# Half of the first layer's embedding projection, made at the end of attention

## The chip, the cores and the metric

The kernel runs on one core of a Trainium2 chip. The metric is the device time of one execution in microseconds (us). Before the change three runs took 1222.86 to 1224.16 us, median 1223.41 us.

## The reference

Two layers over 512 tokens of width 1024, all in fp32. The first layer mixes with forgetting attention (16 heads of 64), the second with a short gated convolution; each is followed by a squared-ReLU MLP and by a gated embedding.

```python
for i in range(DEPTH):                       # DEPTH = 2
    g = norm_g[i]
    hn = rmsnorm(x, g[0])
    m = fox_attention(hn, ...) if i % 2 == 0 else short_conv(hn, ...)
    x = x + rmsnorm(m, g[1])
    f = sq_relu_mlp(rmsnorm(x, g[2]), w_mlp_up[i], w_mlp_down[i])
    x = x + rmsnorm(f, g[3])
    gate = jax.nn.sigmoid(rmsnorm(x, g[4]) @ w_ple_gate[i])
    e = (p[i] @ w_ple_proj[i]) * gate        # p[i]: 512 x 256, w_ple_proj[i]: 256 x 1024
    x = x + rmsnorm(e, g[5])
```

The change concerns `p[i] @ w_ple_proj[i]` for i = 0. It depends on inputs alone.

## The kernel before

Tokens are cut into four blocks of 128 (t) and the width into two halves of 512 columns (n). Every fp32 product is made of three matmuls on operands split into a high and a low part: `mm3` issues high x high (L266), high x low (L267) and low x high (L268). A split is a cast on ScalarE (ACT, L274) and a subtraction on VectorE (DVE, L275) or GpSimd (POOL); of a weight it gives `wh` and `wl`, which are pages.

All buffers in SBUF of 128 x 512 fp32 come from one pool of 70 pages. Results of matmuls go to eight PSUM banks of 128 x 512. Weights are read in one planned order (`plan`): `fetch` issues the load on SyncE's queue into one of 14 `raw` buffers, and `prepare` splits. `wide(key, soon=n)` gives a split weight and sees that the n that come after it in the plan are split as well.

Which instruction stands where in an engine's queue is decided by a scheduler when the program is built; each queue is then worked through in that order. In some stretches the order is that of the code (`manual_schedule`).

The stages of the first layer that matter here:

- *Attention.* For each head, score matmuls (`sc`, L542) are turned into probabilities on DVE, ACT and POOL; these are turned by TensorE (PE) into `pT` (L561), split into `ph` (ACT) and `pl` (DVE), and mixed with the values into `ps_o` (L583, L584). When a head is done, ACT copies half of its bank (`o`, L588) and DVE adds the other half into `oT` (L589); `oT` is later split into `hTh` and `hTl`. A loop over c issues the turn of piece c, the mix of piece c - LAG, and the scores of a piece that is SCORED later; between these it takes steps from a generator, `stream`, which fills TensorE: first the query and key projections of the later heads (`project`, 16 steps for each of seven, 112 in all), then 28 steps of the output projection (`out_part`, one `mm3` each). `share` says how many steps are to be done by piece c; LEFT = 10 steps stay for after the loop.
- *Output projection, MLP.* The rest of the output projection (`o`) and its norm follow, then the MLP (`up`, `dn`), in which TensorE has no gap.
- *The gate's stage* (`ple`). `proj(t, n)` makes one block of p times its weights: six matmuls (`pp`) into a bank. The first four of the eight blocks in BLOCKS, (0,0), (1,0), (0,1), (1,1), are made ahead of the gate matmuls (`early`), while the last results of the MLP are normed and turned (`n_p`, L325). For each block then come 24 gate matmuls (`pg`), a sigmoid on ACT, `proj` if it was not early, the product `e` on DVE (L1069), squares, gain and residual; after both halves of a block its next norm begins, and the second layer's conv (`c`, `u`, `b`) follows.

Of the kernel before, what the change touches and what calls it, by code (L numbers as in the profile page):

```python
# [17 lines left out]
S = 512  # L18
# [8 lines left out]
LAG = 2  # L27
# [53 lines left out]
def trunk(ctx: ExitStack, tc, g4T, x, xT, pT, g, g0T, wv, wqk, bf, wo, wci, wcs, wcb, cw, wco, wup, wdn, wpp, wpg, out):  # L81
# [13 lines left out]
    def bank(name):  # L95
        return psum.tile([P, S], F32, tag="ps", name=name)
# [15 lines left out]
    def plan(key, src):  # L112
        where[key] = len(order)
        order.append((key, len(loads)))
        loads.append(src)
# [60 lines left out]
    def wide(*key, soon=SOON):  # L176

        prepare(where[key] + 1 + soon)
        return ready[key]

    behind = {}
    sums_w = {n: dram.tile([3, P, 2 * S], F32, tag=f"ws{n}", name=f"ws{n}") for n in SUMS_W}

    sum_steps = [(name, kind, i) for name, kind in SUM_STEPS for i in range(3)]
# [21 lines left out]
    for l in range(2):  # L206
        if l == 0:
            for c, (_, width) in enumerate(V_CHUNKS):
                for k in range(KT * width // 512 if width < 272 else KT):
                    plan(("v", c, k), wv[c][k])  # L210
            for i in range(KT):
                for j in range(4):
                    plan(("qk", i, j), wqk[i, j])
            for k in range(KT):
                for n in range(2):
                    plan(("o", n, k), wo[n, k])
        else:
            for s, key in enumerate((("cu", 0), ("b", 0), ("cu", 1))):
                for j in range(4):
                    plan((*key, j), wci[s, j])  # L220
            for i in range(2, KT, 2):
                for _, _, n in PARTS:
                    src = sums_w[n] if n in sums_w else wcs[QUARTERS.index(n)]
                    for s in range(2):
                        plan(("sq", i, s, n), src[i // 2 - 1][:, s * S : (s + 1) * S])
                for j in range(4):
                    plan(("b", i, j), wcb[i // 2 - 1, j])
            for n in range(2):
                for k in range(KT):
                    plan(("co", n, k), wco[n, k])  # L230
        for gr in range(8):
            for i in range(2):
                for j in range(4):
                    plan(("up", l, 2 * gr + i, j), wup[l, 2 * gr + i, j])
            if gr < 7:
                plan_down(l, gr)
                continue
            for n in range(2):
                for f in range(4):
                    plan(("dn", l, gr, n, f), wdn[l, n, 4 * gr + f])  # L240
        for k in range(2):
            plan(("p", l, k), pT[l, :, k, :])
        for n in range(2):
            for k in range(2):
                plan(("pp", l, n, k), wpp[l, n, k])
        for n in range(2):
            for k in range(KT):
                plan(("pg", l, n, k), wpg[l, n, k])
# [130 lines left out]
    def tokens_of(pair, t):  # L379
        return pair.at(lambda h: h[:, t * P : (t + 1) * P])  # L380
# [26 lines left out]
    def attention(hT, first_xT, g0_col, first_x, by_hand):  # L407
# [201 lines left out]
        def out_part(ts, ks):  # L609

            streaming.clear()
            split_o()
            for k in ks:
                for t in ts:
                    for n in range(2):
                        if (t, n) not in banks_o:
                            banks_o[t, n] = bank(f"o{n}_{t}")
                        w = wide("o", n, k, soon=O_SOON)
                        mm3(banks_o[t, n], tokens(oT[0], k, t), w, k == 0, False)
                        yield  # L620

        def stream():
            for i in range(1, KT):
                yield from project(i)
            yield from out_part((0,), range(6))
            yield from out_part((1,), range(6))
            prepare(where["o", 1, KT - 1] + 1)
            yield from out_part((0, 1), (6,))
# [90 lines left out]
        for c in range(-SCORED, n_sc + LAG):  # L719
            if c == n_sc - BY_HAND:  # L720
                by_hand.enter_context(tc.manual_schedule(engines={E.PE}))
            last = n_sc - SCORED - 8
            share = (
                2 * (c + SCORED + 1) if c < last
                else 112 + (c - last + 1) * (28 - LEFT) // (SCORED + 7 + LAG)
            )
            while done < max(share + AHEAD, min(share + STACK, 112)):
                next(main, None)
                done += 1
            if 0 <= c < n_sc:  # L730
                turn(c // 4, c % 4)
            if c >= LAG:
                mix((c - LAG) // 4, (c - LAG) % 4)
            if c % 2 == 0 and c + SCORED < n_sc:
                scores((c + SCORED) // 8, (c + SCORED) % 8 // 2)
            for h in range(2, H):
                if c == 8 * (h // 2) - SCORED - (7 if h % 2 == 0 else 4):
                    bias(h)
# [271 lines left out]
    def ple(l, hT, xs, rs, gB, then):  # L1010
        def proj(t, n):
            pe = bank(f"pp{l}_{n}_{t}")
            for k in range(2):
                mm3(
                    pe, tokens_of(wide("p", l, k), t),
                    wide("pp", l, n, k), k == 0, k == 1,
                )
            return pe
# [29 lines left out]
                )  # L1048
                then(t, at, q)

        early = [proj(t, n) for t, n in BLOCKS[:EARLY]]
        mgs, sums = {}, {}
        for t, n in BLOCKS:
            need(t)
            if (t, n) == (2, 0):
                prepare(where["pg", l, 1, KT - 1] + 1 + SOON)
            pe = early.pop(0) if early else None
            if l == 1 and (t, n) == BLOCKS[-1]:
                last(t, n, mgs[t, 1 - n], sums[t, 1 - n])
                break  # L1060
            ps = bank(f"pg{l}_{n}_{t}")
            for k in range(KT):
                w = wide("pg", l, n, k, soon=soon(t, n))
                mm3(ps, tokens(hT, k, t), w, k == 0, k == KT - 1)
            gate = page(f"gate{l}_{n}_{t}")
            nc.scalar.activation(gate[:, :S], ps, AF.Sigmoid, scale=rs[t])
            pe = pe or proj(t, n)
            e = page(f"e{l}_{n}_{t}")
            nc.vector.tensor_tensor(out=e[:, :S], in0=pe, in1=gate[:, :S], op=ALU.mult)  # L1069
            sums[t, n] = squares(e[:, :S], f"es{l}_{n}_{t}")  # L1070
            mgs[t, n] = gained(e[:, :S], gB, n, f"em{l}_{n}_{t}")
            if (t, 1 - n) in mgs:
                residual(t, *([d.pop((t, i)) for i in range(2)] for d in (mgs, sums)), xs[t],
                         f"er{l}")
                if l == 0:
                    sum_weights()
                then(t)
                if l == 0:
                    sum_weights()
# [145 lines left out]
```

## Time and profile before

| | |
|---|---|
| three runs | 1222.86 to 1224.16 us, median 1223.41 us |
| profiled execution | 1221.69 us, span of its instructions 1220.0 us |
| busy in the span | PE 1207.2, DVE 899.1, ACT 692.1, POOL 658.7 us |
| mean granted TensorE clock | 0.999 |
| attention, up to the last mixing matmul | to 221.2 us |
| rest of the output projection | to 253 us |
| first MLP | 253 to 587.6 us |
| gate's stage of the first layer | 587.7 to 646.6 us |

Rows of the timeline give the start in us from the span's beginning, the length in us, engine, line and operation, tiles (out<-in) and shape, and in brackets how long the engine sat idle before and what ended that. Rows of windows give for a stretch its length, then the busy time and count of PE, PE's weight loads, DVE, ACT and POOL, the granted clock, the DMA share and GB/s. Rows of a tile give the line, engine, operation, count, the least, middle and greatest length in ns, the first and last start, and the shapes.

### The profile page before, as it was taken

Reading aid. Unit: us, or ns where it says so; the run is one execution under the profiler, and the core shown is the slowest. Engines: PE = TensorE matmul, PEld = TensorE weight load, DVE = VectorE, ACT = ScalarE, POOL = GpSimd, SP = SyncE. Lnnn points to the kernel's source line nnn. Section 1 sums busy time; section 2 is a strip of 40 time slices with the busy share of each in tenths; the row PEclk is TensorE's granted clock in tenths of the full one; section 3 lists DMA queues with packets and bytes.
Section 4 is the critical chain, followed back from the end, with each engine's and each line's share of the span. In section 5 each row is a group of like instructions: output and inputs, shape, how many; then the busy total and the mean of one; then the engine's idle time right before and its main releaser. Section 6 shows DMA issues by size and latency. Waiting matters only on the chain.

```text
span 1220.0 us, 18646 instructions
## 1 busy us (share of the span) xinstructions
PE 1207.2 (99%) x6200; PEld 1030.9 (84%) x6200; DVE 899.1 (74%) x1380; ACT 692.1 (57%) x1424; POOL 658.7 (54%) x674
## 2 busy tenths in 40 slices
PE   9999999999999999999999999999999999999997
PEld 8888887898888888888889999889888888888886
DVE  5668888675679776879757877656777687669953
ACT  7567887558634563456756544345756445645641
POOL 3057666167887788775311000028777878678220
PEclk9999999999999999999999999999999999999999
DMA  9554442622365656538345344622422343235401
GB/s 312 192 175 133 128 132 63 218 96 81 104 190 155 156 133 174 161 95 268 105 138 131 111 151 151 192 96 70 138 74 83 120 139 99 67 112 184 144 18 52
DMA packets 90417, 162.90 MB, mean 134 GB/s; under 512 B 10704, under 2 KB 17920, under 8 KB 90128
## 3 DMA queue, kind: packets, MB, share of 16 engines
q1 hardware_dynamic: 86528, 148.85, 38.3%
q0 software_dynamic: 3648, 12.58, 4.8%
q8 instruction: 49, 0.80, 0.3%
q14 instruction: 48, 0.39, 0.1%
q10 hardware_dynamic: 144, 0.26, 0.1%
HBM read 155.29 MB, written 18.96 MB: 143 GB/s over the span
## 4 chain that ended last, share of the span: by engine, by line
PE 95%; DVE 2%; ACT 2%; issue 1%; POOL 0%; POOLq 0%; DVEq 0%; ACTq 0%
PE up L267 9%; PE up L268 9%; PE up L266 9%; PE dn L268 9%; PE dn L266 8%; PE dn L267 8%; PE pg L268 2%; PE pg L266 2%; PE pg L267 2%; PE qk L266 2%; PE qk L267 2%; PE qk L268 2%; PE sq L268 2%; PE sq L267 2%; PE sq L266 2%; PE sc L542 1%
## 5 line engine op out<-in xcount | busy, mean ns | idle before, releaser
L275 DVE TENSOR_TENSOR wl<-raw,wh 128x512 fp32r<-128x512 f32 (+1 forms) x390 | 365.5, 982 | 28.4 <-ACT wh L274 24.3
L274 ACT CAST wh<-raw 128x512 fp32r<-128x512 f32 (+1 forms) x390 | 212.8, 618 | 10.0 <-DMA raw<-in_wv 3.7
L267 PE MATMUL up<-hTl,wh 128*128 128x512 f32 (+1 forms) x576 | 209.9, 366 | 0.0
L266 PE MATMUL up<-hTh,wh 128*128 128x512 f32 (+1 forms) x576 | 209.3, 366 | 0.0
L268 PE MATMUL up<-hTh,wl 128*128 128x512 f32 (+1 forms) x576 | 209.0, 365 | 0.0
L275 POOL TENSOR_TENSOR wl<-T,wh 128x512 fp32r<-128x512 f32 x112 | 157.5, 1438 | 25.9 <-ACT wh L274 24.6
L903 ACT ACTIVATE r<-up 128x512 f32<-128x512 f32 (+1 forms) x72 | 39.4, 547 | 197.0 <-PE up L268 197.0
L951 DVE TENSOR_TENSOR acc<-dn,acc 128x512 f32<-128x512 f32 x168 | 107.8, 678 | 34.7 <-PE dn L268 34.7
L267 PEld LDWEIGHTS up<-hTl,wh 128*128 128x128 f32 x576 | 108.6, 189 | 17.4
L266 PEld LDWEIGHTS up<-hTh,wh 128*128 128x128 f32 x576 | 108.3, 189 | 17.7
L268 PEld LDWEIGHTS up<-hTh,wl 128*128 128x128 f32 x576 | 108.6, 189 | 17.4
L149 POOL TENSOR_TENSOR T<-raw,raw 128x512 f32<-128x512 f32 x56 | 88.5, 1593 | 55.6 <-DMA raw<-in_wdn 23.4
L149 POOL TENSOR_TENSOR T<-raw,T 128x512 f32<-128x512 f32 x56 | 90.7, 1619 | 2.2
L296 POOL TENSOR_SCALAR cor_r_v<-cos,cos 128x1 f32<-128x1 f32 x4 | 1.6, 396 | 152.5 <-ACT junk L308 152.5
L274 ACT CAST wh<-T 128x512 fp32r<-128x512 f32 x112 | 61.4, 616 | 7.0 <-POOL T L149 7.0
L275 DVE TENSOR_TENSOR A11l<-q,A11h 128x256 fp32r<-128x256 f32 x28 | 27.3, 976 | 40.3 <-ACT A11h L274 40.3
L275 DVE TENSOR_TENSOR A12l<-q,A12h 128x512 fp32r<-128x512 f32 x28 | 26.4, 943 | 39.6 <-ACT A12h L274 39.6
L958 POOL TENSOR_TENSOR acc<-acc,acc 128x512 f32<-128x512 f32 x28 | 47.0, 1712 | 10.0 <-DVE acc L951 10.0
L266 PE MATMUL pg<-wh,hTh 128*128 128x512 f32 (+1 forms) x136 | 51.9, 381 | 0.0
L268 PE MATMUL pg<-wh,hTl 128*128 128x512 f32 (+1 forms) x136 | 51.4, 378 | 0.0
L267 PE MATMUL pg<-wl,hTh 128*128 128x512 f32 (+1 forms) x136 | 51.3, 377 | 0.0
L266 PE MATMUL qk<-hTh,wh 128*128 128x512 f32 x128 | 50.9, 398 | 0.0
(318 smaller groups left out, 3267.6 us busy)
## 6 DMA issues: line engine op xcount, KB each, us to landing
raw<-in_wup SPq DMA_DIRECT2D x128, 256.0 KB, 2.8
raw<-in_wdn SPq DMA_DIRECT2D x128, 256.0 KB, 2.8
wst<-in_wcs POOLq DMA_DIRECT2D x18, 512.0 KB, 5.4
raw<-in_wqk SPq DMA_DIRECT2D x32, 256.0 KB, 4.8
raw<-in_wpg SPq DMA_DIRECT2D x32, 256.0 KB, 3.7
raw<-wst SPq DMA_DIRECT2D x24, 256.0 KB, 3.0
g<-in_g SPq DMA_DIRECT2D x18, 256.0 KB, 6.0
raw<-in_wcs SPq DMA_DIRECT2D x18, 256.0 KB, 2.9
```

What stands on the lines that cost most here:

```text
L149: nc.gpsimd.tensor_tensor(out=B[name, p], in0=B[a, p], in1=B[b, p], op=ALU.subtract)
L266: nc.tensor.matmul(ps, a.hi, b.hi, start=start, stop=False)
L267: nc.tensor.matmul(ps, a.hi, b.lo, start=False, stop=False)
L268: nc.tensor.matmul(ps, a.lo, b.hi, start=False, stop=stop)
L274: nc.scalar.copy(hi, src)
L275: eng.tensor_tensor(out=lo, in0=src, in1=hi.bitcast(F32), op=ALU.subtract)
L296: nc.gpsimd.tensor_scalar(out=v, in0=parts[0], scalar1=parts[1], scalar2=EPS, op0=ALU.add, op1=ALU.add)
L542: nc.tensor.matmul(ps[:, :nm], at[:, b * P : n], to[:, :nm], start=s == 0, stop=s == 1)
L903: nc.scalar.activation(r[:, :n], ps[:, :n], AF.Relu)
L951: nc.vector.tensor_tensor(out=a, in0=banks[s], in1=a, op=ALU.add)
L958: nc.gpsimd.tensor_tensor(out=a, in0=a, in1=acc[i, s][:, :S], op=ALU.add)
```

## The change

The four blocks of the second half (n = 1) of the first layer's p times weights are made by a new generator, `embed_part`, as eight more steps of `stream` between the last `project` and the output projection. Each block gets a bank `ppa`, and ACT copies it into a page `ahead`, which is kept until the gate's stage. There the product `e` reads the page, and `early` holds only (0,0) and (1,0); (2,1) and (3,1) no longer call `proj`. For this p is loaded and split a second time, and the two weight tiles of the half stand in the plan ahead of the output projection's. `share` counts eight more steps up to the end of the loop; LEFT is unchanged.

```diff
@@ the plan
                 for j in range(4):
                     plan(("qk", i, j), wqk[i, j])
+            for k in range(2):
+                plan(("pa", l, k), pT[l, :, k, :])
+            for k in range(2):
+                plan(("ppa", l, 1, k), wpp[l, 1, k])
             for k in range(KT):
                 for n in range(2):
                     plan(("o", n, k), wo[n, k])
...
         for n in range(2):
             for k in range(2):
-                plan(("pp", l, n, k), wpp[l, n, k])
+                if l or n == 0:
+                    plan(("pp", l, n, k), wpp[l, n, k])
@@ attention
+        def embed_part():
+
+            streaming.clear()
+            split_o()
+            for t in range(NB):
+                ps = bank(f"ppa_{t}")
+                for k in range(2):
+                    mm3(
+                        ps, tokens_of(wide("pa", 0, k, soon=O_SOON), t),
+                        wide("ppa", 0, 1, k, soon=O_SOON), k == 0, k == 1,
+                    )
+                    yield
+                ahead[t, 1] = page(f"ahead{t}")
+                nc.scalar.copy(ahead[t, 1][:, :S], ps)
+
         def stream():
             for i in range(1, KT):
                 yield from project(i)
+            yield from embed_part()
             yield from out_part((0,), range(6))
...
             share = (
                 2 * (c + SCORED + 1) if c < last
-                else 112 + (c - last + 1) * (28 - LEFT) // (SCORED + 7 + LAG)
+                else 112 + (c - last + 1) * (36 - LEFT) // (SCORED + 7 + LAG)
             )
-            while done < max(share + AHEAD, min(share + STACK, 112)):
+            while done < max(share + AHEAD, min(share + STACK, 120)):
@@ ple
-        early = [proj(t, n) for t, n in BLOCKS[:EARLY]]
+        early = {(t, n): proj(t, n) for t, n in BLOCKS[:EARLY] if (l, n) != (0, 1)}
...
-            pe = early.pop(0) if early else None
+            pe = early.pop((t, n), None)
+            if l == 0 and n == 1:
+                pe = ahead.pop((t, n))[:, :S]
...
-            pe = pe or proj(t, n)
+            if pe is None:
+                pe = proj(t, n)
```

The scheduler orders both programs anew. Lines of the changed kernel are higher by 5 in the helpers and in attention up to the new function (L266 is now L271, L542 is L547), and by more behind it. Three places show what moved.

TensorE's queue at the end of attention, before, at the scores of the seventh pair of heads (`pT_1` is the turn of a piece of an earlier head, `ps_o` the mix):

```order
L542 MATMUL sc_2_2796<-kh_6_2233,q_6_2230 128x384
L542 MATMUL sc_2_2796<-kl_6_2234,q_6_2230 128x384
L561 MATMUL pT_1_2833<-ident,pr_2097 128x128
L561 MATMUL pT_1_2833<-ident,prr_2099 128x128
L561 MATMUL pT_1_2833<-ident,prl_2098 128x128
L583 MATMUL ps_o_2733<-ph_2_2729,v_2_175 128x256
L584 MATMUL ps_o_2733<-pl_2_2730,v_2_175 128x256
L561 MATMUL pT_2_2846<-ident,prr_2099 128x128
L561 MATMUL pT_2_2846<-ident,prl_2098 128x128
L583 MATMUL ps_o_2733<-ph_3_2764,v_2_179 128x256
L584 MATMUL ps_o_2733<-pl_3_2765,v_2_179 128x256
L583 MATMUL ps_o_2853<-ph_0_2789,v_2_167 128x512
```

The same place of the change:

```order
L547 MATMUL sc_2_2796<-kh_6_2233,q_6_2230 128x384
L547 MATMUL sc_2_2796<-kl_6_2234,q_6_2230 128x384
L271 MATMUL ppa_2841<-wh_2306,wh_2238 128x512
L272 MATMUL ppa_2841<-wl_2307,wh_2238 128x512
L273 MATMUL ppa_2841<-wh_2306,wl_2239 128x512
L271 MATMUL ppa_2841<-wh_2328,wh_2263 128x512
L272 MATMUL ppa_2841<-wl_2329,wh_2263 128x512
L273 MATMUL ppa_2841<-wh_2328,wl_2264 128x512
L588 MATMUL ps_o_2733<-ph_2_2729,v_2_175 128x256
L589 MATMUL ps_o_2733<-pl_2_2730,v_2_175 128x256
L566 MATMUL pT_1_2848<-ident,pr_2097 128x128
L566 MATMUL pT_1_2848<-ident,prr_2099 128x128
```

The first block of six stands directly behind the scores; a second stands between the mixes with `ph_3` and `pl_3` of the same head, and the third and fourth follow within the 42 rows that begin with the first `ppa`. The output projection's first matmul stood six rows behind the last row shown of before's queue; now it stands 37 rows behind the last `ppa`.

ACT's queue at the same place, before:

```order
L274 CAST ph_1_2837<-pT_1_2833 128x384
L588 COPY o_2843<-ps_o_2733 64x512
L552 ACTIVATE prr_2514,sm_2_2809<-prr_2514,nmx_2_2808 128x384
L274 CAST ph_2_2849<-pT_2_2846 128x256
L274 CAST hTh<-oT_2585 128x512
L552 ACTIVATE prl_2400,sm_3_2864<-prl_2400,nmx_3_2863 128x512
L552 ACTIVATE prl_2513,sm_3_2871<-prl_2513,nmx_3_2870 128x512
L274 CAST ph_3_2897<-pT_3_2895 128x128
```

and of the change:

```order
L279 CAST ph_1_2852<-pT_1_2848 128x384
L593 COPY o_2858<-ps_o_2733 64x512
L557 ACTIVATE prr_2514,sm_2_2809<-prr_2514,nmx_2_2808 128x384
L640 COPY ahead_2863<-ppa_2841 128x512
L279 CAST ph_2_2875<-pT_2_2872 128x256
L279 CAST hTh<-oT_2585 128x512
L640 COPY ahead_2903<-ppa_2865 128x512
L557 ACTIVATE prl_2400,sm_3_2890<-prl_2400,nmx_3_2889 128x512
L640 COPY ahead_2922<-ppa_2905 128x512
L279 CAST ph_3_2914<-pT_3_2912 128x128
L279 CAST ph_0_2933<-pT_0_2928 128x512
L557 ACTIVATE prl_2513,sm_3_2897<-prl_2513,nmx_3_2896 128x512
```

Three of the four copies stand among the casts and exponentials of three heads, and the second `prl` exponential has moved behind two casts; the fourth copy stands nine rows further.

TensorE's queue at the start of the gate's stage, before, at the end of the early blocks:

```order
L268 MATMUL pp_1_1_7238<-wh_6923,wl_6855 128x512
L325 MATMUL n_p_0_7242<-ident,xd_1_0_6778 128x128 x4
L266 MATMUL pp_1_1_7238<-wh_6935,wh_6866 128x512
L325 MATMUL n_p_1_7249<-ident,xd_1_1_6780 128x128 x4
L267 MATMUL pp_1_1_7238<-wl_6936,wh_6866 128x512
L268 MATMUL pp_1_1_7238<-wh_6935,wl_6867 128x512
L266 MATMUL pg_0_0_7259<-wh_6957,hTh 128x512
L267 MATMUL pg_0_0_7259<-wl_6958,hTh 128x512
```

and of the change:

```order
L273 MATMUL pp_0_1_7284<-wh_6938,wl_6915 128x512
L271 MATMUL pp_0_1_7284<-wh_6950,wh_6926 128x512
L272 MATMUL pp_0_1_7284<-wl_6951,wh_6926 128x512
L273 MATMUL pp_0_1_7284<-wh_6950,wl_6927 128x512
L271 MATMUL pg_0_0_7291<-wh_6983,hTh 128x512
L272 MATMUL pg_0_0_7291<-wl_6984,hTh 128x512
L330 MATMUL n_p_0_7307<-ident,xd_1_0_6838 128x128 x4
L330 MATMUL n_p_1_7314<-ident,xd_1_1_6840 128x128 x4
```

The gate's first matmul stands twelve matmuls nearer to the MLP's last, and the turn of the second token block, which stood among the early blocks, now stands behind the gate's second matmul.

More of the change, by code (lines that the diff above doesn't have):

```diff
@@ L179, in wide @@
         return ready[key]
-    behind = {}
+    behind, ahead = {}, {}
     sums_w = {n: dram.tile([3, P, 2 * S], F32, tag=f"ws{n}", name=f"ws{n}") for n in SUMS_W}
```

## The prediction

> **What bounds the kernel now.** I read the head of the page, then the chain of waits, then TensorE's own timeline, because the first two name one engine and the third says how full it really is.
>
> ```profile
> span 1220.0 us, 18646 instructions
> PE 1207.2 (99%) x6200; PEld 1030.9 (84%) x6200; DVE 899.1 (74%) x1380; ACT 692.1 (57%) x1424; POOL 658.7 (54%) x674
> PE 95%; DVE 2%; ACT 2%; issue 1%; POOL 0%; POOLq 0%; DVEq 0%; ACTq 0%
> ```
>
> TensorE (PE) carries 95% of the chain. A change that only moves matmuls can therefore win only what TensorE loses somewhere, and the busy sum seems to leave 12.8 us over the whole span. But a matmul's row is longer than the room it takes. In a stretch where nothing is waited for:
>
> ```profile
> 195.11 0.28 PE L542 MATMUL sc<-kh,q 128*128 128x256 f32 x1
> 195.47 0.28 PE L542 MATMUL sc<-kl,q 128*128 128x256 f32 x1
> 204.35 0.27 PE L561 MATMUL pT<-ident,pr 128*128 128x128 f32 x1
> 204.46 0.27 PE L561 MATMUL pT<-ident,prr 128*128 128x128 f32 x1
> 222.60 0.39 PE L266 MATMUL o<-wh,hTh 128*128 128x512 f32 x1
> 226.00 0.39 PE L266 MATMUL o<-wh,hTh 128*128 128x512 f32 x1
> ```
>
> Fifteen matmuls of 512 columns start between 222.60 and 226.00, so one takes 0.227 us of the engine, though its row says 0.39. Likewise a 256-column one takes 0.12 (three steps in 0.36) and a transpose 0.11; for 384 columns I estimate 0.175, halfway between 0.12 and 0.227. So a gap up to about 0.16 us long behind a matmul counts as busy, and I count starts instead. The place that matters is the end of attention, from the last matmul ahead of the new ones (184.3) to the last mixing matmul (221.2):
>
> ```profile
> 184.30:221.30 37.00, 35.25 (x191) 27.86 (x190) 29.92 (x82) 27.05 (x67) 20.48 (x36) 1.00 0.15 47
> L266 PE MATMUL o<-wh,hTh x20: 387/393/478, 188.9 to 220.1; 128*128 128x512 f32 x20
> L267 PE MATMUL o<-wl,hTh x20: 389/394/501, 189.1 to 220.3; 128*128 128x512 f32 x20
> L268 PE MATMUL o<-wh,hTl x20: 389/394/481, 189.4 to 220.5; 128*128 128x512 f32 x20
> L542 PE MATMUL sc<-kh,q x11: 281/367/411, 183.9 to 201.7; 128*128 128x512 f32 x4, 128*128 128x256 f32 x4, 128*128 128x384 f32 x3
> L542 PE MATMUL sc<-kl,q x11: 283/332/398, 184.1 to 202.0; 128*128 128x512 f32 x4, 128*128 128x256 f32 x4, 128*128 128x384 f32 x3
> L561 PE MATMUL pT<-ident,prl x23: 270/272/328, 184.8 to 219.6; 128*128 128x128 f32 x23
> L561 PE MATMUL pT<-ident,prr x22: 270/272/327, 184.7 to 217.5; 128*128 128x128 f32 x22
> L561 PE MATMUL pT<-ident,pr x11: 270/273/328, 184.5 to 217.0; 128*128 128x128 f32 x11
> L583 PE MATMUL ps_o<-ph,v x26: 274/364/504, 184.8 to 221.0; 128*128 128x256 f32 x14, 128*128 128x512 f32 x6, 128*128 128x384 f32 x6
> L584 PE MATMUL ps_o<-pl,v x26: 278/361/470, 185.0 to 221.1; 128*128 128x256 f32 x14, 128*128 128x512 f32 x6, 128*128 128x384 f32 x6
> ```
>
> The first row's columns after the length are busy time and count of PE, weight loads, DVE, ACT and POOL. Of 512 columns there are 60 + 8 + 12 = 80, of 256 28 + 8 = 36, of 384 12 + 4 = 16 (the two at 183.9 and 184.1 lie before), of 128 56. Room needed: 80 x 0.227 + 36 x 0.12 + 16 x 0.175 + 56 x 0.11 = 31.4 us of 36.9. TensorE loses **5.5 us** here, where its busy row admits 1.75. DVE and ACT are busy 81% and 73%: this is the stretch in which TensorE waits for the softmax pieces. One cluster can be seen directly:
>
> ```profile
> 185.22 0.27 PE L561 MATMUL pT<-ident,prl 128*128 128x128 f32 x1
> 185.51 0.39 PE L583 MATMUL ps_o<-ph,v 128*128 128x256 f32 x1
> 186.25 0.36 PE L584 MATMUL ps_o<-pl,v 128*128 128x256 f32 x1 [0.35 <-DVE pl L275]
> 187.35 0.50 PE L583 MATMUL ps_o<-ph,v 128*128 128x512 f32 x1 [0.74 <-ACT ph L274]
> ```
>
> Start to start 0.29, 0.74 and 1.10 where 0.11, 0.12 and 0.12 would do: 1.8 us lost in three steps.
>
> The Trainium skill, "Trainium Kernel Development and Optimization", section "Performance Expectations", says that matmul busy time is a bad metric, since matmuls are pipelined. The trace agrees (0.39 against 0.227); by the busy row the change could gain 1.75 us at most, by starts 5.5.
>
> **The change, part by part.** *Removed from the gate's stage:* four blocks of six matmuls, two at its start and two inside. 24 x 0.227 = **5.4 us** of TensorE. Is the stage TensorE's?
>
> ```profile
> 587.60:646.60 59.00, 59.00 (x282) 49.16 (x282) 38.62 (x59) 36.00 (x79) 16.35 (x26) 1.00 0.36 105
> 587.66 0.39 PE L266 MATMUL pp<-wh,wh 128*128 128x512 f32 x1
> 593.99 0.39 PE L266 MATMUL pg<-wh,hTh 128*128 128x512 f32 x1
> 590.40 0.68 DVE L275 TENSOR_TENSOR hTl<-n_p,hTh 128x512 fp32r<-128x512 f32 x1
> 600.04 1.42 DVE L368 SCALAR_TENSOR_TENSOR xd<-acc,mr_r_y,xd 128x512 f32<-128x512 f32 x2 [0.85 <-POOL mr_r_y L303]
> 605.14 1.03 PE L325 MATMUL n_p<-ident,xd 128*128 128x128 f32 x8
> 646.59 0.28 PE L266 MATMUL c<-hTh,wh 128*128 128x256 f32 x1
> ```
>
> Yes: between 587.66 and 646.59 the starts follow without a gap worth naming, and DVE and ACT have a third of it free. Two covers get thinner. The early blocks end 2.7 us sooner, at about 590.4; the gate's first matmul then needs the first half of the turned tokens, whose second half is complete at 590.40 + 0.68 = 591.1 and is asked for four weight tiles (4 x 0.68 us) later. And the turn of the last token block, at 605.14 before and at 605.3 after (counting the room of the rows ahead of it in the new order), needs a DVE row that is finished at 601.5. Neither becomes late, so the whole 5.4 us leaves this stage, and conv begins 5.4 us earlier.
>
> *Added at the end of attention:* the same 24 matmuls, 5.4 us of TensorE, in the stretch that loses 5.5. The new order puts them into 42 rows that begin directly ahead of the cluster above, twelve of them before the matmuls that waited there, so its 1.8 us are filled for certain. The other 3.6 us of added work pushes TensorE back, and it is filled only as far as the later waits then find their pieces ready. Against that stand new pieces on the two engines waited for: four copies out of PSUM on ACT, and, since the eight splits made ahead now include p and its weights, three more o splits before the last mix.
>
> ```profile
> 630.29 1.18 ACT L1153 COPY hp<-n0b_p 128x512 f32<-128x512 f32 x2 [0.27 <-DVE hTl L275]
> L274 ACT CAST wh<-raw 128x512 fp32r<-128x512 f32 x5 | 3.1, 619 | 0.0
> L275 DVE TENSOR_TENSOR wl<-raw,wh 128x512 fp32r<-128x512 f32 x5 | 3.9, 773 | 0.3 <-ACT wh L274 0.3
> ```
>
> ACT: 4 x 0.59 + 3 x 0.62 = 4.2 us; DVE: 3 x 0.77 = 2.3 us. They raise DVE from 29.9 to 32.2 and ACT from 27.1 to 31.3 of 37, so neither is full; but they stand in queues, with `pl` and `ph` behind them, which the mixing matmuls wait for. If all of ACT's 4.2 delays them, the 3.6 is lost and 0.6 more: gain 1.8 - 0.6 = 1.2. If none does, the gain is 5.4. I take DVE's 2.3 in full, because `pl` is the later of the two pieces, and ACT's as hidden, because ACT is idle for 10 us here: 3.6 - 2.3 = 1.3 filled beside the 1.8. **Gain 3.1 us.**
>
> The Trainium skill, "SBUF — State Buffer", section "Who interferes with whom", says that a DVE instruction with two SBUF inputs is blocked by a GpSimd instruction that reads SBUF. One split in this stretch agrees:
>
> ```profile
> 209.35 1.13 DVE L275 TENSOR_TENSOR wl<-raw,wh 128x512 fp32r<-128x512 f32 x1 [0.26 <-ACT wh L274]
> 209.25 1.57 POOL L554 TENSOR_SCALAR prl<-prl,rs 128x512 f32<-128x512 f32 x1 [0.23 <-DVE rs L553]
> ```
>
> By it each of the three splits could cost 0.36 us more (1.13 against 0.77), 1.1 in all, and the gain would be 2.0, the time 1221.4, inside the forecast's own range. The four products that now read a page and not PSUM have two such inputs too, in a stage where DVE has 20 us free.
>
> *Two more loads and splits* (p is loaded and split twice) lie before 184 in the places where o's stood: the order there is the same row by row, so they cost nothing; without that cover one split is 0.77.
>
> **Sum.** The profiled execution took 1221.69 us (span 1220.0), the three runs 1222.86 to 1224.16 with median 1223.41. A gain of 3.1 makes 1218.6 of the one and **1220.3** of the median, its own range 1218.8 to 1222.0.
>
> **The rivals.** That the matmuls stand elsewhere than said is out: the order shows them. *All of it fits* (0.14): the 5.5 us of room take the 5.4 whole, since DVE keeps 4.8 us free. Time 1218.0. Against it: queues are in order, and what ACT copies delays `ph`. *The end of attention is DVE's and ACT's* (0.26): what TensorE does between is free already, and the copies push the last turn back; then only the idle time of the busy row, 1.75 us, or less is won: 1221.7 to 1223.4. For it: where the new matmuls go in, DVE is busy 98% and ACT 90% of the time.
>
> ```profile
> 184.30:189.00 4.70, 3.58 (x18) 2.38 (x17) 4.61 (x15) 4.25 (x10) 3.96 (x10) 1.00 0.25 82
> ```
>
> *The pages* (0.08): four of 70 are held through the whole first MLP, and splits of weights could wait for a page.
>
> ```profile
> 500.00:560.00 60.00, 60.00 (x266) 49.71 (x265) 48.71 (x56) 28.71 (x53) 48.40 (x35) 1.00 0.47 146
> L275 DVE TENSOR_TENSOR wl<-raw,wh x101: 672/1184/1786, 292.7 to 559.7; 128x512 fp32r<-128x512 f32 x101
> PEld dn L268 <- DVE A12l L275: 0.2, 1, 0.2
> ```
>
> Here DVE is 81% busy, and a split takes 1.18 us. One late split in each of seven groups costs 7 x 1.18 = 8.3, and the kernel is slower: 1223.4 - 3.1 + 8.3 = 1228.6. It decides from 0.44 us a group. Against it: TensorE's only wait between 280 and 560 is the 0.2 us of the last row, and the order of DVE, ACT and POOL through this MLP is unchanged.
>
> **Chances.** The forecast has 0.52. A measurement here tells about 0.2%, 2.45 us, from no change. Of the forecast 0.39 lies beyond that and 0.13 within; the full fit adds 0.14 to faster; the third case gives 0.24 to same and 0.02 to slower; the pages 0.08 to slower. So faster 0.53, same 0.37, slower 0.10. The range 1217.3 to 1224.2 takes in the full fit and the third case, with 0.7 at each end for the spread of the runs (1.3 from end to end), and leaves out the pages.
>
> **What would show it.** Right: the gate's stage, from its first early matmul to conv's first, takes 53.5 us where it took 58.9; and from the last matmul ahead of the new ones to the last mixing matmul it is 39.9 us: 36.9, the 2.3 that are not filled, and 0.7 for three o matmuls that stood behind it before. At 37.6 all of it fits; at 41.3 or more (3.7 not filled), with longer waits on `ph`, the third case is right. Waits of TensorE on `wl` between 260 and 585 would show the pages. A gate stage that shrinks by less than 5 us would make the first term wrong.

## The result and the profile after

The changed kernel takes **1220.49 us** (median of 12 runs, 1219.47 to 1221.74), the kernel before 1222.78 us beside it (12 runs, 1222.08 to 1224.89). The ratio is 0.9981, 95% interval 0.9974 to 0.9989: 2.3 us or 0.19% faster; 3.1 us and 1220.3 were forecast, so the time lies well within the forecast's own range. A second set of runs of the same kernel gave 0.9979 (0.9970 to 0.9988), 2.6 us. The effect is real and sits on the edge of the 0.2% that the prediction set as its bound.

The head of the page and the chain of the changed kernel (profiled execution 1220.50 us):

```profile
span 1218.8 us, 18668 instructions
PE 1206.4 (99%) x6200; PEld 1031.6 (85%) x6200; DVE 901.0 (74%) x1382; ACT 693.5 (57%) x1430; POOL 656.2 (54%) x674
PE 93%; DVE 2%; ACT 2%; issue 1%; POOL 0%; POOLq 0%; DVEq 0%; ACTq 0%
```

The page shows the change nowhere: TensorE has the same 6200 matmuls and 99%. The stages show it. TensorE's timeline at the two ends of the first layer's gate stage:

```profile
592.23 0.39 PE L271 MATMUL pp<-wh,wh 128*128 128x512 f32 x1
...
645.76 0.28 PE L271 MATMUL c<-hTh,wh 128*128 128x256 f32 x1
```

That is 53.53 us where it was 58.93, **5.40 us** less. The place where two waits stood one behind the other (185 to 187 us):

```profile
185.14 0.34 PE L547 MATMUL sc<-kl,q 128*128 128x384 f32 x1
185.48 0.50 PE L271 MATMUL ppa<-wh,wh 128*128 128x512 f32 x1
...
186.75 0.39 PE L273 MATMUL ppa<-wh,wl 128*128 128x512 f32 x1
186.97 0.28 PE L588 MATMUL ps_o<-ph,v 128*128 128x256 f32 x1
187.09 0.28 PE L589 MATMUL ps_o<-pl,v 128*128 128x256 f32 x1
```

Six new matmuls stand there, and the mixing matmuls behind them no longer wait. The rest of the end of attention, with the waits that are left, and the last mixing matmul:

```profile
198.58 0.39 PE L588 MATMUL ps_o<-ph,v 128*128 128x256 f32 x1 [0.35 <-ACT ph L279]
199.34 0.33 PE L547 MATMUL sc<-kl,q 128*128 128x384 f32 x1
...
208.65 0.50 PE L589 MATMUL ps_o<-pl,v 128*128 128x512 f32 x1
...
221.32 0.50 PE L588 MATMUL ps_o<-ph,v 128*128 128x512 f32 x1 [0.38 <-DVE pl L280]
...
225.49 0.28 PE L589 MATMUL ps_o<-pl,v 128*128 128x256 f32 x1
```

From the last matmul ahead of the new ones (185.14) to 225.49 it is **40.35 us**, for 36.95 before; 39.9 were forecast. One output step (three matmuls, 0.68 us) more than before lies in it, so 5.46 us of new matmuls lengthened the path by 40.35 - 36.95 - 0.68 = 2.7 us, and 2.7 were filled. By these two stages the change is worth -5.4 + 2.7 = -2.7 us. The two profiled executions as wholes differ by 1.2 us only (1221.69 and 1220.50): the changed kernel's came 1.0 us later to 185 us and was 0.8 us longer in the first MLP. Both parts vary by as much, or nearly, between executions in which their order is the same (184.15 to 185.20 us at the first, 334.9 to 335.5 us for the second).

It helps to cut this stretch in two, at its last score matmul of 384 columns. TensorE's room is counted as the prediction did, from the number of matmuls of each width (0.2275, 0.175, 0.119 and 0.109 us); "lost" is the length less the room. The rows of the ends and of the cut in the profile before, and both windows of each kernel (columns: length, busy time and count of PE, weight loads, DVE, ACT, POOL; before, then after):

```profile
184.15 0.33 PE L542 MATMUL sc<-kl,q 128*128 128x384 f32 x1
...
199.66 0.34 PE L542 MATMUL sc<-kl,q 128*128 128x384 f32 x1
...
221.10 0.28 PE L584 MATMUL ps_o<-pl,v 128*128 128x256 f32 x1
```

```profile
184.15:199.66 15.51, 14.39 (x80) 11.62 (x79) 12.89 (x42) 11.91 (x33) 12.34 (x23) 1.00 0.08 27
199.66:221.10 21.44, 20.81 (x111) 16.05 (x111) 17.18 (x41) 15.23 (x36) 8.29 (x14) 1.00 0.21 62
```

```profile
185.14:199.34 14.20, 13.84 (x79) 11.44 (x78) 12.40 (x40) 12.49 (x34) 11.82 (x22) 1.00 0.08 29
199.34:225.50 26.16, 25.75 (x140) 21.45 (x140) 19.63 (x48) 17.91 (x43) 8.78 (x15) 1.00 0.30 91
```

| | first half: length, room, lost | second half: length, room, lost | output matmuls in it |
|---|---|---|---|
| before | 15.51, 13.00, **2.51** | 21.44, 18.39, **3.05** | 24 and 36 |
| after | 14.20, 12.88, **1.32** | 26.15, 24.65, **1.50** | 0 and 63 |

The new matmuls did not simply come on top. In the first half 24 of them took the place of 24 output matmuls, and could start at 185.48, ahead of the waits, where the output matmuls had started at 188.92. The output matmuls moved back: the second half has 27 more of them, these 24 and three (one step) that stood behind the stretch before. One mixing matmul of 256 columns has moved over the cut as well, hence the small difference of room in the first half.

### The profile page after: what moved, and what is told of

The parts are those of the page before. It is cut to its first block, busy times and chain, and to the rows that moved or that the text cites. A ratio compares the mean times of both kernels' runs of the same rounds, so it can differ in the third digit from the quotient of the medians.

```text
span 1218.8 us, 18668 instructions
## 1 busy us (share of the span) xinstructions
PE 1206.4 (99%) x6200; PEld 1031.6 (85%) x6200; DVE 901.0 (74%) x1382; ACT 693.5 (57%) x1430; POOL 656.2 (54%) x674
## 4 chain that ended last, share of the span: by engine, by line
PE 93%; DVE 2%; ACT 2%; issue 1%; POOL 0%; POOLq 0%; DVEq 0%; ACTq 0%
PE up L271 9%; PE up L272 9%; PE up L273 9%; PE dn L273 8%; PE dn L271 8%; PE dn L272 8%; PE pg L273 2%; PE pg L272 2%; PE pg L271 2%; PE qk L271 2%; PE qk L272 2%; PE qk L273 2%; PE sq L273 2%; PE sq L272 2%; PE sq L271 2%; PE sc L547 1%
## 5 line engine op out<-in xcount | busy, mean ns | idle before, releaser
L271 PE MATMUL up<-hTh,wh 128*128 128x512 f32 (+1 forms) x576 | 209.3, 366 | 0.0
L924 ACT ACTIVATE r<-up 128x512 f32<-128x512 f32 (+1 forms) x72 | 39.4, 547 | 196.7 <-PE up L273 189.7
L271 PEld LDWEIGHTS up<-hTh,wh 128*128 128x128 f32 x576 | 108.3, 189 | 17.6
L280 DVE TENSOR_TENSOR A11l<-q,A11h 128x256 fp32r<-128x256 f32 x28 | 28.5, 1017 | 40.3 <-ACT A11h L279 40.3
L271 PE MATMUL pg<-wh,hTh 128*128 128x512 f32 (+1 forms) x136 | 51.8, 381 | 0.0
L271 PE MATMUL qk<-hTh,wh 128*128 128x512 f32 x128 | 50.9, 398 | 0.0
```

What stands on the lines that cost most here:

```text
L271: nc.tensor.matmul(ps, a.hi, b.hi, start=start, stop=False)
L280: eng.tensor_tensor(out=lo, in0=src, in1=hi.bitcast(F32), op=ALU.subtract)
L924: nc.scalar.activation(r[:, :n], ps[:, :n], AF.Relu)
```

## The experiments

All were run beside the kernel before (1222.5 to 1222.8 us). "The stretch" is the one above: from the last 384-column score matmul ahead of the new ones to the last mixing matmul.

**The two terms apart.** The gate's stage without its four blocks (and without the two loads and splits of their weights), nothing added:

```diff
-        early = [proj(t, n) for t, n in BLOCKS[:EARLY]]
+        early = {(t, n): proj(t, n) for t, n in BLOCKS[:EARLY] if (l, n) != (0, 1)}
+        if l == 0:
+            stand_in = page("stand_in")
+            nc.gpsimd.memset(stand_in[:, :S], 1.0)
...
+            if l == 0 and n == 1:
+                pe = stand_in[:, :S]
```

> The kernel before without the four blocks of p times the weights' second half in the first layer's gate stage: their 24 matmuls and the two loads and splits of those weights are left out, and one page of ones stands in for the product. Nothing is added at the end of attention. The prediction's first term (24 x 0.227 us, whole, since the stage is TensorE's): 5.4 us less than before, about 1217.4 us. Rival (a thinner cover makes a turn or a split late, so that part of it is given back): 4.4 us less or fewer.

Measured: 1218.52 us, ratio 0.9964 (0.9952 to 0.9976, five runs): 4.3 us less, between 2.9 and 5.9. By its median the run meets the rival's mark (4.4 or fewer), though the interval takes in the forecast's 5.4 too. The stage itself decides it:

```profile
589.99 0.39 PE L267 MATMUL pp<-wh,wh 128*128 128x512 f32 x1
...
643.46 0.28 PE L267 MATMUL c<-hTh,wh 128*128 128x256 f32 x1
```

53.47 us, 5.46 less than before: nothing is given back there. Of what the profiled execution lacks, 1.4 us is a slow run of matmuls at 188 us (last section); how much of the median it explains is not known. And the end of attention alone, the gate's stage as before:

```diff
-                if l or n == 0:
-                    plan(("pp", l, n, k), wpp[l, n, k])
+                plan(("pp", l, n, k), wpp[l, n, k])
...
-            if l == 0 and n == 1:
-                pe = ahead.pop((t, n))[:, :S]
```

> The changed kernel whose end of attention is unchanged (24 matmuls, four copies, two more loads and splits of p), but whose gate stage makes all eight blocks again as before and reads no page; the pages are so free again at once. The prediction's sum: 5.4 us of TensorE added, 1.8 + 1.3 filled, so 2.3 us more than before, about 1225.1 us. The two traces as compared so far (2.7 of 5.4 filled): 2.7 us more, 1225.5. All fits: 1222.8. The end of attention is DVE's and ACT's: 3.7 more or above, 1226.5. The pages: together with the run that only takes from the gate stage, this gives less than 2.3 us of gain if holding four pages costs nothing, and the sum of both differences lies below the changed kernel's by the price of the pages if it costs something.

Measured: 1225.98 us, ratio 1.0025 (1.0015 to 1.0035): 3.2 us more, between 1.8 and 4.3; the stretch takes 40.24 us. Both terms have the forecast's sign, and in the traces its size (5.46 for 5.4; 2.6, without the one output step more, for 2.3). Holding the pages costs nothing to be seen: the two differences add up to -1.1 us, the change gives -2.3, and a price of the pages would have made it the other way round, though the two intervals together leave about 2 us open either way. The trace is the finer measure: the first MLP, from its first matmul to the gate's stage, took 334.9 to 335.5 us in five executions that hold the four pages through it and 334.2 to 335.3 in four that do not.

**DVE's splits.** The prediction had three extra ones, lost in full. Here the second piece of every output weight is its first piece again, so DVE makes none of these splits:

```diff
+            if key[0] == "o":
+                hi = page(f"wh{n}", F32R)
+                fetch(at + 1)
+                nc.scalar.copy(hi[:, :S], fetched[at][:, :S])
+                fetched[at] = None
+                ready[key] = Pair(hi[:, :S], hi[:, :S])
+                continue
```

> The changed kernel without DVE's half of the splits of attention's output weights: the second piece of a weight tile is the first piece again, so DVE makes none of these 16 instructions (nine of them stand before the last mixing matmul) and the numbers in the second product are not the reference's. The prediction's step (three splits of 0.77 us on DVE push the last turn back in full): at least 2.3 us faster than the changed kernel, 1218.2 us or less. Rival (DVE's splits are covered, since DVE is idle for 2.6 us ahead of the last pieces, and what isn't filled comes from elsewhere): within 0.6 us of the changed kernel, 1219.9 to 1220.5.

Measured: 1218.48 us (five runs, 0.9967, 0.9954 to 0.9979), 2.0 us less than the changed kernel's first set and 1.4 less than its second. By the time alone the step looked nearly right (1218.2 or less was its mark). The stretch says otherwise:

```profile
184.10 0.34 PE L554 MATMUL sc<-kl,q 128*128 128x384 f32 x1
...
223.65 0.28 PE L596 MATMUL ps_o<-pl,v 128*128 128x256 f32 x1
```

39.55 us for 40.3, 0.75 us for all nine of DVE's pieces, not 2.3 for three. The rest of the difference lies in other stages: this execution came to the stretch 1.0 us sooner than the changed kernel's and was 0.6 us shorter in the MLP. The run leaves out four such splits ahead of the stretch and three behind it too; whether they give part of this, or chance does, is not known.

**ACT's copies.** The prediction had them hidden. Here only the first block is copied:

```diff
-                ahead[t, 1] = page(f"ahead{t}")
-                nc.scalar.copy(ahead[t, 1][:, :S], ps)
+                ahead[t, 1] = ahead[0, 1] if t else page("ahead0")
+                if t == 0:
+                    nc.scalar.copy(ahead[t, 1][:, :S], ps)
```

> The changed kernel with one of the four copies out of PSUM on ACT: the other three blocks' products are computed and not kept, and the gate's stage reads the first block's page four times. The prediction's step (ACT's copies are hidden in its idle time): same as the changed kernel within 0.4 us, 1220.1 to 1220.9. Rival (the copies stand in ACT's queue ahead of the pieces that TensorE waits for): 3 x 0.59 = 1.8 us faster, 1218.7.

Measured: 1219.21 us (six runs, 0.9969, 0.9957 to 0.9981), between the two expected values. The stretch takes 39.61 us, 0.7 less, and all of it in the first half, where the wait on `ph` at 198 us is gone:

```profile
184.53:197.81 13.28, 13.28 (x78) 11.39 (x78) 12.19 (x39) 11.52 (x32) 11.94 (x22) 1.00 0.10 29
```

13.28 us, 0.40 lost, for 14.20 and 1.32. So three copies of 0.59 us cost 0.9 us there (0.2 of it comes back in the second half), and ACT is not hidden.

**Both left out, and the changed kernel again.**

> The changed kernel without DVE's half of the splits of attention's output weights and with one of the four copies on ACT (two parts left out together, numbers not the reference's). If DVE's pieces alone cause what isn't filled (the prediction's step): as without the DVE halves, end of attention 39.55 us, within 0.3. If each of DVE's pieces and ACT's copies costs 0.7 us by itself: 38.8 us, 1.5 us less than the changed kernel's 40.3. If both delay the same pieces, one after the other in two queues: 39.2 to 39.6. The floor by TensorE's own room is 37.5 us.

> The changed kernel once more, unaltered, as the measure for the runs beside it and as a second profile: 1220.5 us, and 40.3 us from the last matmul ahead of the new ones to the last mixing matmul, as in the two executions seen of this order (40.35 and 40.24).

Measured: 1218.45 us (five runs, 0.9967, 0.9954 to 0.9979) with a stretch of 39.36 us, and 1219.92 us (0.9979) with one of 40.30. Two pieces of 0.7 and 0.75 us give 0.95 together: they overlap. Even without them TensorE loses 1.8 us.

**The pieces without the matmuls.** The eight steps of the new generator stay, and are empty:

```diff
-                    mm3(
-                        ps, tokens_of(wide("pa", 0, k, soon=O_SOON), t),
-                        wide("ppa", 0, 1, k, soon=O_SOON), k == 0, k == 1,
-                    )
+                    wide("pa", 0, k, soon=O_SOON)
+                    ps = wide("ppa", 0, 1, k, soon=O_SOON).hi.bitcast(F32)
                     yield
```

> The changed kernel without the 24 matmuls at the end of attention, but with all that comes with them: the two more loads and splits of p, the order of the eight splits made ahead, and four copies on ACT (of a piece of the weights that lies in SBUF, since nothing is in PSUM to be copied); the kept pages hold no product. TensorE's room in the end of attention is then 32.1 us instead of 37.5. If the copies and splits set the length (the third case of the prediction, and its step that DVE's splits are lost in full): 39.5 us or more from the last 384-column score matmul to the last mixing matmul, nearly the 40.3 of the changed kernel, so that the matmuls themselves cost next to nothing. If the matmuls set it and the pieces are covered: 37.6 us as in the profile before (36.95 and one output step more), 38.2 at most; the whole is then 2.2 us faster than the changed kernel. A fall of TensorE's clock after the two waits at 185 to 187 us, which are open again here, would add 1.4 us.

Measured: 1219.88 us (0.9978, 0.9969 to 0.9987), no faster than the changed kernel, and a stretch of 40.21 us. Its two halves:

```profile
184.46:197.35 12.89, 10.58 (x54) 7.45 (x54) 11.98 (x38) 11.87 (x33) 11.34 (x22) 1.00 0.12 33
197.35:224.70 27.35, 26.45 (x140) 21.49 (x140) 20.15 (x49) 18.73 (x44) 9.18 (x15) 1.00 0.30 87
```

Without the 5.46 us of matmuls the first half is 1.3 us shorter, and the second half, with the same matmuls as in the changed kernel, 1.2 us longer. Taken alone this says that the pieces set the length. But the empty steps keep one thing of the change: the output matmuls are still pushed back into the second half.

**The matmuls without the pieces.** The 24 matmuls are made of the output weights' tiles, so no p is loaded or split ahead, and nothing is copied:

```diff
-                        ps, tokens_of(wide("pa", 0, k, soon=O_SOON), t),
-                        wide("ppa", 0, 1, k, soon=O_SOON), k == 0, k == 1,
+                        ps, tokens_of(wide("o", 0, k, soon=O_SOON), t),
+                        wide("o", 1, k, soon=O_SOON), k == 0, k == 1,
...
-                ahead[t, 1] = page(f"ahead{t}")
-                nc.scalar.copy(ahead[t, 1][:, :S], ps)
+                ahead[t, 1] = every_one
```

> The complement of the run with pieces only: the changed kernel with its 24 matmuls at the end of attention, made on the first four tiles of attention's output weights, which are split there anyway, so that no p and no weights of it are loaded or split ahead (the eight splits made ahead are the output weights' again, as before the change), and with no copy on ACT; nothing is kept, and a page of ones stands in for the product in the gate's stage. TensorE's room in the end of attention is the changed kernel's, 37.5 us. If the pieces set its length (as the run with pieces only says, 40.2 us without any of the matmuls): 39.4 us or less from the last 384-column score matmul to the last mixing matmul, that is what is left without copies and without DVE's splits (39.36) or below, down to the prediction's upper bound of all that fits, 37.6. If the matmuls set it: 40.2 us again.

Measured: 1220.28 us (0.9981, 0.9972 to 0.9990), and a stretch of 39.75 us: neither 39.4 or less nor 40.2. Its ends and the cut:

```profile
185.38 0.34 PE L543 MATMUL sc<-kl,q 128*128 128x384 f32 x1
...
198.63 0.34 PE L543 MATMUL sc<-kl,q 128*128 128x384 f32 x1
...
225.13 0.28 PE L585 MATMUL ps_o<-pl,v 128*128 128x256 f32 x1
```

The first half loses 0.37 us now, the second 1.85. So neither the new matmuls nor their copies and splits set the length by themselves: without the one it is 40.2 us, without the other 39.75. What both runs share is the second half, with 63 output matmuls in it and 26.5 to 27.3 us long.

**Output matmuls as the filler.** The kernel before, with `LEFT = 2` for 10:

> The kernel before with one number changed: LEFT = 2 for 10, so that eight more steps of attention's output matmuls (24 matmuls of 512 columns, 5.4 us, as many as the change moves) are asked for before the last mixing matmul; no copies, no pages, no loads. If any filler does (what counts is 5.4 us of matmuls in a stretch that loses 5.5): 2.3 us faster than before, 1220.5. If it matters where the filler stands (the order shows these matmuls from about 199 us on, behind the two waits at 185 to 187 that lose 1.8 us): 1.0 us faster at most, 1221.8 to 1222.8. A second question: whether TensorE's clock falls after those two waits, as it did in one of two executions of this order (0.51 from 188 to 191.5 us, 1.4 us lost).

Measured: 1225.29 us, ratio 1.0019 (1.0010 to 1.0028): *slower* than before by 2.3 us (2.8 by the medians), worse than either theory. The second half gets 24 more matmuls (5.46 us) and goes from 21.44 to 26.22 us; and then the output stage, short of steps whose pieces are ready, waits for the last head:

```profile
227.46 0.28 PE L584 MATMUL ps_o<-pl,v 128*128 128x256 f32 x1
229.84 0.50 PE L266 MATMUL o<-wh,hTh 128*128 128x512 f32 x1 [2.10 <-ACT hTh L274]
```

Not any filler does. The two waits at 185 to 187 us stay open here, since no output matmul stands ahead of them.

**Fewer output matmuls.** The changed kernel, with `LEFT = 14` for 10:

> The changed kernel with one number changed: LEFT = 14 for 10, so that four fewer steps of attention's output matmuls (12 matmuls, 2.7 us) are asked for before the last mixing matmul. If the end of attention is TensorE's at its end (between 213 and 220 us TensorE has no wait and DVE and ACT idle 2.6 and 2.3 us ahead of the last turn): its length falls by 2.7 us and the output stage grows by 2.7, the time is the same within 0.4 us, 1219.7 to 1220.7. If the fillers are needed there: the waits grow and the time is 0.5 to 1.5 us longer.

Measured: 1219.95 us (0.9978, 0.9969 to 0.9987). The stretch falls to 37.83 us (the second half to 23.68) and the output stage behind it grows from 30.97 to 33.68: the same sum within 0.2 us, as expected of a stretch whose end is TensorE's.

**A block at another wait.** Ahead of the last turn before the first MLP TensorE waits 0.38 and 1.05 us. Three blocks in attention; the fourth is made and copied there by a new function, `embed_last`:

```diff
-            for t in range(NB):
+            for t in range(NB - 1):
                 ps = bank(f"ppa_{t}")
...
             for n in range(2):
+                if name == "n20" and (t, n) == (NB - 1, 1):
+                    embed_last()
                 ps = turned(t, n, hs[n], name)
```

> The changed kernel with three of the four blocks at the end of attention and the fourth (six matmuls, 1.36 us) directly ahead of the last turn before the first MLP, where TensorE waits 0.38 and 1.05 us for DVE. If what counts is that a block stands where TensorE waits: the fourth block is filled whole there, and the end of attention gets 0.7 to 1.4 us shorter: 1219.1 to 1219.8. If the turn is late by other work then (ACT copies the block ahead of the turn's pieces): 1220.5 or above.

Measured: 1219.98 us (0.9979, 0.9970 to 0.9988), the changed kernel's time and neither of the two expected. At its new place the block is hidden:

```profile
265.78 0.63 PE L330 MATMUL n_p<-ident,n_h 128*128 128x128 f32 x4 [0.37 <-DVE n_h L321]
266.17 0.47 PE L271 MATMUL ppa<-wh,wh 128*128 128x512 f32 x1
...
267.63 0.60 PE L330 MATMUL n_p<-ident,n_h 128*128 128x128 f32 x4
```

But the stretch stays at 40.24 us with 1.36 us less in it: 57 output matmuls in the second half, 2.46 us lost there for 1.50. Taking a block out of the stretch did not make it shorter.

**A fifth block there**, from the weights' first half, with two loads and splits of its own ahead of it:

```diff
+            for k in range(2):
+                plan(("ppa", l, 0, k), wpp[l, 0, k])
...
+                if name == "n20" and (t, n) == (NB - 1, 1):
+                    embed_last()
...
-                prepare(where[kind, 1, KT - 1] + 1 + SOON)
+                prepare(where[kind, 1, KT - 1] + 1 + SOON + 2 * (kind == "o"))
```

> The changed kernel with a fifth block moved: the product of the last token block with the weights' first half leaves the gate's stage (six matmuls, 1.36 us) and stands directly ahead of the last turn before the first MLP, where TensorE waits 1.05 us for DVE and the profile loses 1.24; two more loads and splits of those weights lie in the stage of attention's output matmuls, and a fifth page is held. The end of attention is unchanged. If a moved block is worth what TensorE loses at its new place: 1.2 us faster than the changed kernel, 1218.7 to 1219.0; in the profile the gate's stage takes 52.2 us for 53.5 and the first MLP (335.5 us) the same within 0.3. If the splits or the fifth page hold the MLP up: 1220 or above.

Measured: 1222.72 us, ratio 0.9993 (0.9985 to 1.0002): the gain of the change is gone. The gate's stage is 52.17 us, as forecast; the MLP takes 337.5 us, 2.0 more. TensorE's rows and POOL's, of this run, and then POOL's of the changed kernel:

```profile
265.16 1.04 PE L332 MATMUL n_p<-ident,n_h 128*128 128x128 f32 x8
268.52 0.63 PE L332 MATMUL n_p<-ident,n_h 128*128 128x128 f32 x4 [2.33 <-DVE n_h L323]
268.91 0.48 PE L273 MATMUL ppa<-wh,wh 128*128 128x512 f32 x1
```

```profile
265.65 0.30 POOL L303 TENSOR_SCALAR n_r_v<-n_q,n_q 128x1 f32<-128x1 f32 x1 [3.17 <-ACT junk L315]
```

```profile
263.86 0.30 POOL L301 TENSOR_SCALAR n_r_v<-n_q,n_q 128x1 f32<-128x1 f32 x1 [3.17 <-ACT junk L313]
```

The chain of the norm comes 1.8 us later than in the changed kernel (265.65 for 263.86; 2.3 us later when counted from the last mixing matmul) with two more splits ahead of it, so the wait grows, and it grows *ahead* of the block. On DVE the two splits stand between the rows of that chain; that they alone delay it was not tried apart. The profiled execution was among the fastest (1221.33 us); the other 1.4 us of the median are taken up in the last section.

## Why the prediction was right, and where not

**The gate's stage** (5.4 us, whole): right. 5.40 in the changed kernel, 5.46 alone; neither of the two thinner covers became late.

**The room at the end of attention** (5.5 us, where the busy row admits 1.75): right as a bound. 2.7 us were filled, more than the busy row's 1.75. TensorE still loses 2.8.

**"Filled for certain: the cluster's 1.8":** the two waits are gone, but the first half wins only 1.2 (2.51 to 1.32 lost). ACT's copies cost 0.9 there, at the next wait on `ph`. The later waits took 1.55 (3.05 to 1.50), where the prediction had 1.3.

**"DVE's 2.3 in full, ACT's as hidden":** this is the step that failed; the sum came out near by luck, because two errors met. There were four more splits and not three (nine in the stretch, five before), at

```profile
L280 DVE TENSOR_TENSOR wl<-raw,wh x9: 671/675/710, 205.2 to 216.0; 128x512 fp32r<-128x512 f32 x9
```

and all nine together cost 0.75 us. The copies, taken at nothing, cost 0.7. Left out together they give 0.95 of the 2.7 us that are not filled. For the rest the counts point to something that the prediction did not have: the new matmuls stand *in the place of* output matmuls, and 27 of these (6.1 us) come into the second half, whose waits took 1.55 of them. This half is hard to fill: with 60 output matmuls for 36, and no copy, it grew by 4.8 us of 5.5. That is read from the counts and from `LEFT = 2`; no run has the new matmuls in this stretch without the output matmuls moved back.

**Gain 3.1:** 2.7 by the two stages in the profiles, 2.3 (1.3 to 3.2) and 2.6 (1.5 to 3.7) by the runs. The term that was mis-sized is the fill of the end of attention, 3.1 forecast and 2.7 found.

**Each split 0.36 us more**, by the rule of the Trainium skill, "SBUF — State Buffer", section "Who interferes with whom": not here. The row above has 671 to 710 ns for all nine; the 1.13 us of the profile before did not come again. POOL is busy for 8.8 us of that half, but only three of the nine splits ran beside a POOL row that reads SBUF, each time a scaling of probabilities with one full input (`prr<-prr,rs`, `prl<-prl,rs`), and they took 0.71, 0.67 and 0.67. What POOL's row reads seems to decide: in the whole execution of the changed kernel 180 splits of this shape with no POOL row beside them took 0.63 to 0.69 us; 149 that lay for at least 0.5 us beside a POOL row with two full inputs (TENSOR_TENSOR) took 1.77 in the median; 14 beside rows with one (TENSOR_SCALAR) took 0.69 in the median, 1.19 at most.

**p's two more loads and splits cost nothing:** no cost is seen. At the score matmul ahead of the new ones the changed kernel was 1.0 us behind (185.14 for 184.15), but 0.6 of it was there at 12 us, where both orders are the same. Ten executions with p split ahead came there at 184.10 to 185.20, four without at 184.15 to 185.38.

**The rivals.** All fits (37.6 us): out, 40.35. The pages: out; from the turns at 268 us to 585 TensorE's one listed wait is 0.3 us of `dn` for DVE's `A12l`, on no weight. The end of attention is DVE's and ACT's (41.3 or more): not reached, and the wait on `ph` in it is one of 0.35 us. It holds the partial truth that ACT's copies do cost, and that the stretch hardly gets shorter when the matmuls are left out. Whether the last 2.8 us lost are TensorE's order or the turns behind it stays open: leaving out either side alone moved the stretch by 0.1 to 0.6 us.

## What to carry to other kernels

Work that is put ahead of a queue of fillers does not only fill the waits behind it; it pushes those fillers back, and the price is read where *they* end up. Count the room and the loss of a stretch from the starts and the number of matmuls, before and after, and cut it at a point that both kernels have: only then is it seen which part was filled. And a filler that brings loads and splits of its own may delay the very chain whose wait it should fill: with the fifth block's two splits ahead of it, that chain came 1.8 us later.

## What was not expected of the hardware

**TensorE's clock can fall after waits.** In two of four profiled executions in which the two waits at 185 to 187 us were open, the matmuls right behind them were slow. The run with the gate's stage alone, by windows (the granted clock stands behind POOL's count) and by rows:

```profile
188.00:191.50 3.50, 3.50 (x10) 2.72 (x9) 3.37 (x11) 2.87 (x8) 2.76 (x6) 0.51 0.00 0
```

```profile
187.66 0.50 PE L584 MATMUL ps_o<-ph,v 128*128 128x512 f32 x1 [0.74 <-ACT ph L275]
188.00 0.53 PE L543 MATMUL sc<-kh,q 128*128 128x512 f32 x1
188.33 0.63 PE L543 MATMUL sc<-kl,q 128*128 128x512 f32 x1
188.75 0.63 PE L543 MATMUL sc<-kh,q 128*128 128x512 f32 x1
...
191.31 0.49 PE L267 MATMUL o<-wh,hTh 128*128 128x512 f32 x1
191.64 0.39 PE L268 MATMUL o<-wl,hTh 128*128 128x512 f32 x1
```

Start to start 0.43 us for 0.23, seven times: 1.4 us. It happened in the same way with `LEFT = 2` (clock 0.54 from 187.5 to 191, 1.6 us), and in none of the ten profiled executions with the waits filled. The mean clock was 0.997 in both of these executions, and 0.998 or 0.999 in the other two; taken as the sign of such a fall, it says how often in the timed runs: 0.997 in 7 of 11 runs with `LEFT = 2`, whose times are 1224.85 to 1225.98 against 1223.09 to 1225.42, but in 0 of 14, 2 of 27, 2 of 26 and 0 of 15 of the kernel before. The seven lie 1.5 us above the other four in the mean, so the fall would explain about 0.9 of the 2.3 us that `LEFT = 2` lost, and little of what the change won. The version with five blocks, with its wait of 2.33 us, has 0.997 in 4 of 11 runs (1222.72 to 1223.03 us), and 0.999 in four (1221.06 to 1222.09); a fall of the clock behind that wait would fit, but the one profile of it shows none.

**A DVE row can take 2.4 times as long beside POOL.** In the changed kernel the two `n_h` of the last token block, and POOL beside them:

```profile
258.84 1.42 DVE L321 SCALAR_TENSOR_TENSOR n_h<-xb,n_r_y,g 128x512 f32<-128x512 f32 x2 [1.45 <-POOL n_r_y L308]
264.84 3.44 DVE L321 SCALAR_TENSOR_TENSOR n_h<-xb,n_r_y,g 128x512 f32<-128x512 f32 x2 [2.65 <-POOL n_r_y L308]
264.77 2.96 POOL L149 TENSOR_TENSOR T<-raw,raw 128x512 f32<-128x512 f32 x2
```

1.72 us each beside POOL's subtractions, 0.71 beside POOL's rows of 128x1 alone. This agrees with the Trainium skill, "SBUF — State Buffer", section "Who interferes with whom": both rows read two inputs from SBUF. Two rows of 0.71 would be finished 2.0 us sooner, more than the 1.05 us that TensorE waits there for the second.
